# The gate columns of a mixer as seven products per quad, with turned queries cast later

## The chip, the cores and the metric

One core of one Trainium2 chip. The metric is the device time of one execution in microseconds; the kernel before takes 2320.2 us (median of 3 runs, 2319.61 to 2320.4).

## The reference, cut to what matters

Two layers over 512 tokens of 1024 features, all in f32; the kernel holds everything turned (features on the 128 partitions, tokens along the columns). The change lies in the mixer:

```python
u = rmsnorm(h, mix_norm[i])
b_g, c_g, v_c, q_c, kv_c, k_r, g_conv, g_mla = jnp.split(u @ w_in[i], split_pts, axis=-1)
#   widths:  512, 512, 512, 384, 256, 64, 1024, 1024
z = c_g * v_c                                   # short_conv_branch: three taps along the tokens
y = conv_w[0] * z[t-2] + conv_w[1] * z[t-1] + conv_w[2] * z[t]
y_conv = (b_g * y) @ w_conv_out                 # 512 -> 1024
y_mla = mla_branch(q_c, kv_c, k_r, ...)         # norms of q_c and kv_c, rotary parts, 8 heads
merged = jax.nn.sigmoid(g_conv) * y_conv + jax.nn.sigmoid(g_mla) * y_mla
h = h + merged @ w_o[i]
```

Each layer has a feed-forward block before the mixer and one behind it, and a gated per-layer input at its end.

## The kernel before

**Precision and form of a product.** Every f32 operand is split into two fp32r tiles, a high part (a cast on ScalarE, L67 for weights and L190 for activations) and a low part (source minus high part, on VectorE, L68 and L191). A product is then three matmuls (`mm3`, L196): high x high, high x low, low x high. Weights come as halves of 128 x 1024 f32 (512 KB, eight tiles of 128 x 128) through SyncE's queue into one of ten buffers `st` (`Stream.raw`, L45), and are split into one of four pairs `wh`/`wl` (`Stream.split`, L61).

**The mixer** (`mixer`, L517) is written in the order: norm of h and split into `xs` (eight pairs of 128 x 512); projections of kv, of the rotary key and of q; r, the reciprocal root mean square, by which each projection is multiplied on its way out of PSUM; norm and split of kv and the rotary key; then, for four blocks of 128 channels, projections C, V and B (`m0Cp`, `m0Vp`, `m0Bp`), with the tap loop behind them: z = V x C and y x b are multiplied on POOL (L578, L587), the first tap on VectorE (L581). Then come norm and split of q, eight rounds of one gate projection (`m0gcp`, 24 matmuls of 512 columns) and one output of the convolution (`m0cop`, 12), and eight more gate projections (`m0gmp`). Each gate is multiplied by r on VectorE and goes through the sigmoid on ScalarE. Behind the gates the attention runs over four pairs of heads: `qkv` (L608) makes the turned query `q_rope` (L628, its two casts L634 and subtractions L635 right behind it), keys, queries and values; `scores` (L653) and `turn` (L678) follow one pair later.

**The feed-forward block** (`ffn`, L375) computes its gate and up columns by a Strassen form in Winograd's variant: a quad of four weight quarters (`Quad`, L111) and seven half-size products (`step`, L440; `product`, L418). `Halved` (L346) holds the halves of the activations and their sums and differences (tiles `t` and `u`), split like all others. A product is 24 matmuls of 256 columns into a PSUM bank a, b or c; products 1, 6, 7 and 4 gather in bank b, 5 and 3 in c. ScalarE copies a bank out behind products 1, 5 and 6, VectorE adds behind 2, 3 and 7. `Quad.part` (L119) makes the sums of weight quarters on VectorE (L127 to L138) ahead of the split.

**What sets the order.** The code is written in one order; a scheduler of the tile framework then orders the instructions of each engine, allots the buffers of each pool and sets the waits. So the order on an engine is read from the built program. Names there: `wl`, `wh`, `st`, `s` are weights; `m0` and `m1` the mixers of the two layers; `h1` in `m0h1` the second pair of heads.

Of the kernel before, what the change touches and what calls it, by code (L numbers as in the profile page):

```python
# [158 lines left out]
def trunk_kernel(ctx, tc, dims, x, p, positions, gains, rope_c, weights, out):  # L159
# [186 lines left out]
    class Halved:  # L346
# [6 lines left out]
        def row(self, j, xs):  # L353
# [19 lines left out]
            halves_of(split(t24, f"{name}u{j}"), 6, 4)  # L373

    def ffn(l, nm, name, first=False, beside=None, early=False):  # L375
        H = S // 2
# [33 lines left out]


        def quad(n):
            quarters = {f"a{a_ + 1}{b_ + 1}": [(nm + "_w_gu", l, (4 * b_ + k) * P, c0 + (2 * n + a_) * P)
                                               for k in range(4) for c0 in (0, DFF)]
                        for a_ in range(2) for b_ in range(2)}
            todo[n] = {"w": Quad(W, quarters)}

        def product(ps, n, j):  # L418
            hi, lo = todo[n]["w"].part(j)
            for k, (vh, vl) in enumerate(ys[j]):  # L420
                for w in range(2):
                    at = slice((2 * k + w) * P, (2 * k + w + 1) * P)
                    for i, (a_, b_) in enumerate(((hi, vh), (hi, vl), (lo, vh))):
                        nc.tensor.matmul(ps[:, w, :], a_[:, at], b_, start=j in (1, 5, 2) and w + k + i == 0,
                                         stop=w + k + i == 6, skip_group_check=True)

# [12 lines left out]

        def step(n, j):  # L440
            if n not in todo:
                quad(n)
            d = todo[n]
            nn = f"{name}{n}"

            def T(what):
                return G(nn + what).rearrange("p (w t) -> p w t", t=H)

            bank = {1: "b", 6: "b", 7: "b", 4: "b", 5: "c", 3: "c", 2: "a"}[j]
            if j in (1, 5, 2):  # L450
                d[bank] = PS(nn + bank).rearrange("p (w t) -> p w t", t=H)
            ps = d[bank]
            product(ps, n, j)
            if j in (1, 5, 6):
                d[j] = T(f"c{j}")
                nc.scalar.copy(d[j], ps)
            elif j == 4:
                finish(n, 1, 0, ps, T("t"))
            else:
                i, f, c = {2: (1, 0, 0), 3: (6, 0, 1), 7: (5, 1, 1)}[j]  # L460
                nc.vector.tensor_tensor(d[i], ps, d[i], ALU.add)
                finish(n, f, c, d[i], d[i])

# [53 lines left out]
    def mixer(l):  # L517
# [82 lines left out]
        for m in range(KD):  # L600
            ps = proj(W.col("w_in", l, o_gm + m * P, D), xs, f"{name}gmp{m}")
            g = G(f"{name}gm{m}")
            nc.vector.tensor_tensor(g, ps, r, ALU.mult)  # L603
            nc.scalar.activation(g, g, AF.Sigmoid)
            m_b.append(g)
# [295 lines left out]
```

## Time and profile before

| | |
|---|---|
| median of 3 runs | 2320.2 us |
| the profiled execution: time, span | 2319.08 us, 2317.3 us |
| granted TensorE clock | 0.996 |
| busy: TensorE, its weight load, VectorE, ScalarE, POOL | 2294.0, 2051.2, 1791.4, 1064.2, 59.5 us |
| the gates of the first mixer | 451.32 to 560.15 us |
| the gates of the second mixer | 1592.54 to 1701.37 us |
| bytes read from HBM | 223.66 MB, 97 GB/s over the span |

Times of rows are microseconds from the span's start. Busy times of matmuls overlap, since they are pipelined: a record is 0.28 us long for 256 columns and 0.39 for 512, and what a matmul costs is the distance from one start to the next. Operations of VectorE overlap a little in the same way.

### The profile page before, as it was taken

Reading aid. Unit: us, or ns where it says so; the run is one execution under the profiler, and the core shown is the slowest. Engines: PE = TensorE matmul, PEld = TensorE weight load, DVE = VectorE, ACT = ScalarE, POOL = GpSimd, SP = SyncE. Lnnn points to the kernel's source line nnn. Section 1 sums busy time; section 2 is a strip of 40 time slices with the busy share of each in tenths; the row PEclk is TensorE's granted clock in tenths of the full one; section 3 lists DMA queues with packets and bytes.
Section 4 is the critical chain, followed back from the end, with each engine's and each line's share of the span. In section 5 each row is a group of like instructions: output and inputs, shape, how many; then the busy total and the mean of one; then the engine's idle time right before and its main releaser. Section 6 shows DMA issues by size and latency. Waiting matters only on the chain.

```text
span 2317.3 us, 33585 instructions
## 1 busy us (share of the span) xinstructions
PE 2294.0 (99%) x13696; PEld 2051.2 (89%) x13696; DVE 1791.4 (77%) x2483; ACT 1064.2 (46%) x1563; POOL 59.5 (3%) x58
## 2 busy tenths in 40 slices
PE   9999999999999999999999999999999999999997
PEld 7999988888888999998899999888888889999987
DVE  8988779745866988877898787687378679888776
ACT  7444444234544644444564444433245355444455
POOL 0000000200100000000000000001001000000000
PEclk9999999999999999999999999999999999999998
DMA  5333233332122233333223333322321213233341
GB/s 192 112 107 107 94 123 109 100 99 93 37 71 84 74 112 99 109 108 129 73 83 110 102 100 119 119 91 100 101 82 37 82 55 114 98 108 107 120 137 38
DMA packets 64523, 227.94 MB, mean 98 GB/s; under 512 B 7408, under 2 KB 7408, under 8 KB 64368
## 3 DMA queue, kind: packets, MB, share of 16 engines
q1 hardware_dynamic: 63936, 225.47, 29.7%
q8 instruction: 107, 1.75, 0.3%
q14 instruction: 48, 0.39, 0.1%
q10 hardware_dynamic: 432, 0.32, 0.0%
HBM read 223.66 MB, written 2.10 MB: 97 GB/s over the span
## 4 chain that ended last, share of the span: by engine, by line
PE 94%; DVE 4%; ACT 1%; issue 1%; DMA 0%; ACTq 0%; SPq 0%
PE a1pd L198 2%; PE b0pd L198 2%; PE b1pd L198 2%; PE a0pd L198 2%; PE b1pd L199 2%; PE b0pd L199 2%; PE a0pd L199 2%; PE a1pd L199 2%; PE a0pd L200 2%; PE a1pd L200 2%; PE b1pd L200 2%; PE b0pd L200 2%; DVE wl L68 1%; PE e1gp L198 1%; PE e1gp L199 1%; PE e1gp L200 1%
## 5 line engine op out<-in xcount | busy, mean ns | idle before, releaser
L67 ACT CAST wh<-st 128x1024 fp32r<-128x1024 f32 (+1 forms) x463 | 482.6, 1043 | 683.7 <-issue 146.3
L68 DVE TENSOR_TENSOR wl<-st,wh 128x1024 fp32r<-128x1024 f32 (+1 forms) x463 | 568.8, 1229 | 168.9 <-ACT wh L67 167.4
L67 ACT CAST wh<-s 128x1024 fp32r<-128x1024 f32 x78 | 81.9, 1050 | 101.0 <-PE b1pd L199 8.5
L68 DVE TENSOR_TENSOR wl<-s,wh 128x1024 fp32r<-128x1024 f32 x78 | 94.9, 1216 | 0.9 <-ACT wh L67 0.9
L135 DVE TENSOR_TENSOR st<-st,s 128x1024 f32<-128x1024 f32 x39 | 47.7, 1222 | 1.0
L138 DVE TENSOR_TENSOR st<-st,st 128x1024 f32<-128x1024 f32 x39 | 47.5, 1217 | 0.1
L132 DVE TENSOR_TENSOR s<-s,st 128x1024 f32<-128x1024 f32 x39 | 47.5, 1218 | 0.0
L127 DVE TENSOR_TENSOR s<-st,st 128x1024 f32<-128x1024 f32 x39 | 47.4, 1216 | 0.1
L469 DVE SCALAR_TENSOR_TENSOR h<-b0pd,h 128x512 f32<-128x512 f32 x40 | 27.5, 688 | 9.1 <-PE b0pd L200 9.1
L469 DVE SCALAR_TENSOR_TENSOR h<-b1pd,h 128x512 f32<-128x512 f32 x40 | 27.5, 688 | 9.1 <-PE b1pd L200 9.1
L469 DVE SCALAR_TENSOR_TENSOR h<-a1pd,h 128x512 f32<-128x512 f32 x40 | 27.5, 687 | 7.1 <-PE a1pd L200 7.0
L469 DVE SCALAR_TENSOR_TENSOR h<-a0pd,h 128x512 f32<-128x512 f32 x40 | 27.5, 687 | 6.4 <-PE a0pd L200 6.4
L103 POOL MEMSET wh<- 128x256 f32 x4 | 1.1, 312 | 1196.0 <-DVE wl L68 1196.0
L603 DVE TENSOR_TENSOR m1gm<-m1gmp,m1r 128x512 f32<-128x512 f32 x8 | 5.5, 691 | 26.5 <-PE m1gmp L200 26.5
L603 DVE TENSOR_TENSOR m0gm<-m0gmp,m0r 128x512 f32<-128x512 f32 x8 | 5.5, 691 | 26.2 <-PE m0gmp L200 26.2
L595 DVE TENSOR_TENSOR m1gc<-m1gcp,m1r 128x512 f32<-128x512 f32 x8 | 5.4, 689 | 11.3 <-PE m1gcp L200 11.3
L595 DVE TENSOR_TENSOR m0gc<-m0gcp,m0r 128x512 f32<-128x512 f32 x8 | 5.4, 689 | 11.3 <-PE m0gcp L200 11.3
L598 DVE TENSOR_TENSOR m0gc<-m0cop,m0gc 128x512 f32<-128x512 f32 x8 | 5.4, 690 | 8.4 <-PE m0cop L200 8.3
L598 DVE TENSOR_TENSOR m1gc<-m1cop,m1gc 128x512 f32<-128x512 f32 x8 | 5.4, 691 | 8.4 <-PE m1cop L200 8.3
L729 DVE TENSOR_TENSOR m1gm<-m1mop,m1gm 128x512 f32<-128x512 f32 x8 | 5.5, 690 | 6.6 <-PE m1mop L200 6.5
L729 DVE TENSOR_TENSOR m0gm<-m0mop,m0gm 128x512 f32<-128x512 f32 x8 | 5.5, 690 | 6.6 <-PE m0mop L200 6.5
L272 ACT ACT_TABLE_LOAD x8 | 10.3, 1283 | 0.1
(10023 smaller groups left out, 8593.3 us busy)
## 6 DMA issues: line engine op xcount, KB each, us to landing
st<-in_weights SPq DMA_DIRECT2D x416, 512.0 KB, 3.5
st<-in_weights SPq DMA_DIRECT2D x8, 256.0 KB, 5.3
h<-in_x SPq DMA_DIRECT2D x8, 256.0 KB, 5.4
out<-fo SPq DMA_DIRECT2D x8, 256.0 KB, 2.3
e0pi<-in_p SPq DMA_DIRECT2D x2, 256.0 KB, 3.7
e1pi<-in_p SPq DMA_DIRECT2D x2, 256.0 KB, 3.8
pos_i<-in_positions ACTq DMA_DIRECT2D x1, 256.0 KB, 4.4
cols<-in_gains ACTq DMA_DIRECT2D x1, 53.0 KB, 3.0
```

The costliest lines, as they stand in the source:

```text
L67: self.nc.scalar.copy(hi[:, w], src[:, w])
L68: self.nc.vector.tensor_tensor(lo[:, w], src[:, w], hi[:, w].bitcast(F32), ALU.subtract)
L127: tt(self.s, self.a21, self.a22, ALU.add)
L132: tt(self.s, self.s, self.a11, ALU.subtract)
L135: tt(self.a12, self.a12, self.s, ALU.subtract)
L138: tt(self.a11, self.a11, self.a21, ALU.subtract)
L198: nc.tensor.matmul(ps, wh, vh, start=first, stop=False)
L199: nc.tensor.matmul(ps, wh, vl, start=False, stop=False)
L200: nc.tensor.matmul(ps, wl, vh, start=False, stop=last)
L469: nc.vector.scalar_tensor_tensor(h[m], ps, 0.5, h[m], ALU.mult, ALU.add)
L603: nc.vector.tensor_tensor(g, ps, r, ALU.mult)
L729: nc.vector.tensor_tensor(t, mla_ps[m], t, ALU.mult)
```

## The change

It takes the seven-product form out of `ffn` into a class `Sevens` that the feed-forward block and the mixer use, and makes all 16 blocks of gate columns (2048 columns, `o_gc` and `o_gm` follow each other) by four quads of it. The halves of the activations for it (`ys`) are made one row per round of the convolution. The eight outputs of the convolution stand between products of quads 1 to 3. In the last quad the products stand in the order 6, 2, 7, 3, 4 in place of 2, 6, 3, 7, 4; the splits of q, kv and the rotary key, which stood at their norms, come behind its product 7. In the convolution C is multiplied by r squared, V by that product (both on VectorE, straight from PSUM), the first tap moves to ScalarE, y x b moves from POOL to VectorE, and q's norm moves from behind the loop into it. In `qkv` the casts of the turned query come behind the first key and query. The pool of activation tiles grows from 58 to 60 buffers.

```diff
-N_BIG = 58
+N_BIG = 60
...
+    class Sevens:
+        H = S // 2
+        BANK = {1: "b", 6: "b", 7: "b", 4: "b", 5: "c", 3: "c", 2: "a"}
...
+        def step(self, n, j):
...
+            ps = d[bank]
+            self.product(ps, d, j)
+            if j in (1, 5, 6):
+                d[j] = T(f"c{j}")
+                nc.scalar.copy(d[j], ps)
+            elif j == 4:
+                self.done(n, 1, 0, ps, T("t"))
+            else:
+                i, f, c = {2: (1, 0, 0), 3: (6, 0, 1), 7: (5, 1, 1)}[j]
+                nc.vector.tensor_tensor(d[i], ps, d[i], ALU.add)
+                self.done(n, f, c, d[i], d[i])
...
-        kvc = lat_norm(*kvt, "kv")
-        krh, krl = split(rope(krn, cosT, sinT, name + "kr"), name + "kr")
+        kvt = lat_norm(*kvt, "kv")
+        krt = rope(krn, cosT, sinT, name + "kr")
+        ys = Halved("mix", l, name)
...
+        r2 = G(name + "r2")
+        nc.vector.tensor_tensor(r2, r, r, ALU.mult)
         for k in range(CONV // P):
...
-            nc.vector.tensor_tensor(c, ps, r, ALU.mult)
+            nc.vector.tensor_tensor(c, ps, r2, ALU.mult)
...
-            nc.vector.tensor_tensor(z, ps, r, ALU.mult)
-            nc.gpsimd.tensor_tensor(z, z, c, ALU.mult)
+            nc.vector.tensor_tensor(z, ps, c, ALU.mult)
...
-            nc.vector.tensor_scalar(y, z, cw[2], None, ALU.mult)
+            nc.scalar.mul(y, z, cw[2])
...
-            nc.gpsimd.tensor_tensor(y, y, b, ALU.mult)
+            nc.vector.tensor_tensor(y, y, b, ALU.mult)
             yc.append(split(y, f"{name}yc{k}"))
+            ys.row(k, xs)
+            if k == 1:
+                qt = lat_norm(*qt, "q", SCALE)
...
+        def gate(n, f, c, src, t):
+            at = slice(c * (S // 2), (c + 1) * (S // 2))
+            nc.vector.tensor_tensor(t, src, r[:, at].unsqueeze(1).to_broadcast([P, 2, S // 2]), ALU.mult)
+            for w in range(2):
...
+                nc.scalar.activation(gates[i][:, at], t[:, w, :], AF.Sigmoid)
...
+        step = Sevens("w_in", l, name + "g", ys.ys,
+                      lambda n: [[o_gc + (4 * n + 2 * a_ + w) * P for w in range(2)] for a_ in range(2)], gate).step
+        for j in (1, 2, 5, 6, 3):
+            step(0, j)
+        n_last = KD // 2 - 1
+        for n in range(n_last):
+            between = [(lambda m=m: conv_out(m)) for m in range(4 * n - 4, 4 * n)] if n else []
+            order = [(n + 1, 1), (n, 7), (n + 1, 5), (n, 4)]
+            order += [(n + 1, j) for j in ((6, 2, 7, 3, 4) if n + 1 == n_last else (2, 6, 3))]
+            for i, (n_, j_) in enumerate(order):
+                step(n_, j_)
+                if i in (1, 2, 3, 4 if n + 1 == n_last else 5) and between:
+                    between.pop(0)()
+                if (n_, j_) == (n_last, 7):
+                    qc = [split(t, f"{name}qn{k}") for k, t in enumerate(qt)]
+                    kvc = [split(t, f"{name}kvn{k}") for k, t in enumerate(kvt)]
+                    krh, krl = split(krt, name + "kr")
...
             for _, part in parts:
                 part()
+                if part is query0:
+                    q_rope_parts()
```

Three places of VectorE's order in the first mixer (the second has the same). The first is the edge from the convolution to the gates, in the changed kernel; `m0b` is B times r, `m0y` the tap loop's sum, `m0t` and `m0u` half sums, `s` and `st` weight quarters:

```order
L601 TENSOR_TENSOR m0b_4330<-m0Bp_4299,m0r 128x512
L68 TENSOR_TENSOR wl_4464<-s,wh_4463 128x1024
L602 TENSOR_TENSOR m0y_4295<-m0y_4295,m0b_4330 128x512
L138 TENSOR_TENSOR st_4355<-st_4355,st_4357 128x1024
L191 TENSOR_TENSOR m0yc3l<-m0y_4295,m0yc3h 128x512
L68 TENSOR_TENSOR wl_4495<-st_4361,wh_4494 128x1024
L368 TENSOR_TENSOR m0t_4339<-m0x_4337 128x256
L369 TENSOR_TENSOR m0t_4339<-m0y_4338,m0x_4337 128x256
L68 TENSOR_TENSOR wl_4536<-st_4526,wh_4535 128x1024
L370 TENSOR_TENSOR m0u_4340<-m0t_4339,m0x_4337 128x256
L371 TENSOR_TENSOR m0u_4340<-m0y_4338,m0u_4340 128x256
L191 TENSOR_TENSOR m0t3l<-m0t_4339,m0t3h 128x512
```

Before, the convolution's edge had only its own rows, two weight splits and q's norm; now sums of quarters and splits of the first two quads stand among them, and the last half sums behind them.

The second place is the end of the gates, in the changed kernel (`m0g3` is the last quad, `m0qn`, `m0kvn` and `m0kr` the late splits):

```order
L191 TENSOR_TENSOR m0qn0l<-m0qt_3794,m0qn0h 128x512
L424 TENSOR_TENSOR m0g3c_5292<-m0g3c,m0g3c_5292 128x512
L191 TENSOR_TENSOR m0qn1l<-m0qt_3798,m0qn1h 128x512
L613 TENSOR_TENSOR m0g3c_5292<-m0g3c_5292,m0r 128x512
L191 TENSOR_TENSOR m0qn2l<-m0qt_3803,m0qn2h 128x512
L68 TENSOR_TENSOR wl_5591<-st_5588,wh_5590 128x1024
L191 TENSOR_TENSOR m0kvn0l<-m0kvt_3682,m0kvn0h 128x512
L68 TENSOR_TENSOR wl_5736<-st_5733,wh_5735 128x1024
L191 TENSOR_TENSOR m0kvn1l<-m0kvt_3686,m0kvn1h 128x512
L191 TENSOR_TENSOR m0krl<-m0krt_3826,m0krh 128x512
L613 TENSOR_TENSOR m0g3t<-m0g3b,m0r 128x512
```

The three kinds of late splits moved here from the convolution and the first gates; two memsets and the turned query's first row follow.

The third place is the second pair of heads, before:

```order
L68 TENSOR_TENSOR wl_5617<-st_5614,wh_5616 128x1024
L514 TENSOR_TENSOR m0h1qrt_5229<-m0h1qrt_5229,m0h1qrt_5230 128x512
L635 TENSOR_TENSOR m0h1qr_5237<-m0h1qrt_5229,m0h1qr_5237 64x512
L635 TENSOR_TENSOR m0h1qr_5240<-m0h1qrt_5229,m0h1qr_5240 64x512
L191 TENSOR_TENSOR m0h1kn0l<-m0h1kn_5243,m0h1kn0h 128x512
L191 TENSOR_TENSOR m0h1qn0l<-m0h1qn_5254,m0h1qn0h 128x512
L191 TENSOR_TENSOR m0h1kn1l<-m0h1kn_5274,m0h1kn1h 128x512
```

and in the changed kernel:

```order
L191 TENSOR_TENSOR m0h1kn0l<-m0h1kn_5715,m0h1kn0h 128x512
L529 TENSOR_TENSOR m0h1qrt_5707<-m0h1qrt_5707,m0h1qrt_5708 128x512
L191 TENSOR_TENSOR m0h1qn0l<-m0h1qn_5726,m0h1qn0h 128x512
L68 TENSOR_TENSOR wl_6027<-st_6024,wh_6026 128x1024
L674 TENSOR_TENSOR m0h1qr_5746<-m0h1qrt_5707,m0h1qr_5746 64x512
L674 TENSOR_TENSOR m0h1qr_5749<-m0h1qrt_5707,m0h1qr_5749 64x512
L191 TENSOR_TENSOR m0h1kn1l<-m0h1kn_5752,m0h1kn1h 128x512
```

Between the sum of the turned query (`qrt`) and the subtractions that need ScalarE's cast of it, the first query's split and a weight split have moved.

## Rows read from the trace of the kernel before

**Rows 1.** The page: busy time, share of the span and instructions of each engine, and the chain that ended last by engine.

```profile
PE 2294.0 (99%) x13696; PEld 2051.2 (89%) x13696; DVE 1791.4 (77%) x2483; ACT 1064.2 (46%) x1563; POOL 59.5 (3%) x58
...
PE 94%; DVE 4%; ACT 1%; issue 1%; DMA 0%; ACTq 0%; SPq 0%
```

**Rows 2.** The waits of TensorE: who waited <- for whom: us in total, times, longest.

```profile
PE a0pg L198 <- ACT a0x0h L193: 5.3, 1, 5.3
PE fss L808 <- DVE f0acc L259: 2.6, 1, 2.6
...
PE m0s10p L664 <- DVE m0h1v0l L191: 0.6, 1, 0.6
...
PE m0s20p L664 <- DVE m0h2kn1l L191: 0.3, 1, 0.3
...
PE m0s30p L664 <- DVE m0h3kn1l L191: 0.3, 1, 0.3
```

**Rows 3.** The first mixer's convolution, gates and attention in stretches: the stretch, its us, then busy us (instructions) of PE, PEld, DVE, ACT and POOL, granted clock, DMA share, GB/s.

```profile
385.55:451.32 65.77, 65.77 (x291) 54.43 (x290) 51.18 (x62) 19.30 (x24) 11.53 (x7) 1.00 0.28 94
451.32:560.15 108.83, 108.83 (x481) 90.09 (x480) 51.33 (x56) 32.93 (x41) 1.29 (x1) 1.00 0.30 99
560.15:655.40 95.25, 93.92 (x556) 83.66 (x554) 85.19 (x207) 56.68 (x135) 14.94 (x16) 1.00 0.16 50
```

**Rows 4.** The timeline of TensorE at the first gate matmul and at the first of the turned query, in both layers: start, us, engine, line, operation, tiles, shape.

```profile
451.32 0.39 PE L198 MATMUL m0gcp<-m0x0h,wh 128*128 128x512 f32 x1
...
560.15 0.39 PE L198 MATMUL m0h0qr<-m0qn0h,wh 128*128 128x512 f32 x1
...
1592.54 0.39 PE L198 MATMUL m1gcp<-m1x0h,wh 128*128 128x512 f32 x1
...
1701.37 0.39 PE L198 MATMUL m1h0qr<-m1qn0h,wh 128*128 128x512 f32 x1
```

**Rows 5.** The timeline of TensorE in the second feed-forward block of the first layer: the first matmul of the first product of its first quad, and of the ninth and the twelfth product; then one weight load of such a product (duration min/median/max in ns).

```profile
769.77 0.28 PE L424 MATMUL b01b<-b0x0h,wh 128*128 128x256 f32 x1
...
794.18 0.28 PE L424 MATMUL b01b<-b0u0h,wh 128*128 128x256 f32 x1
...
802.82 0.28 PE L424 MATMUL b02c<-b0x4h,wh 128*128 128x256 f32 x1
```

```profile
L424 PEld LDWEIGHTS b01b<-b0u0h,wh x4: 192/192/192, 778.3 to 794.4; 128*128 128x128 f32 x4
```

**Rows 6.** The timeline of VectorE in the same block: rows of 512, 1024 and 256 columns, each with the next.

```profile
801.26 0.68 DVE L461 TENSOR_TENSOR b02c<-b02a,b02c 128x512 f32<-128x512 f32 x1
801.86 1.21 DVE L68 TENSOR_TENSOR wl<-st,wh 128x1024 fp32r<-128x1024 f32 x1
802.99 0.68 DVE L431 TENSOR_TENSOR b02c<-b02c,b0r 128x512 f32<-128x512 f32 x1
...
804.73 0.42 DVE L436 TENSOR_TENSOR b0an<-b02c 128x256 f32<-128x256 f32 x1
805.07 1.22 DVE L127 TENSOR_TENSOR s<-st,st 128x1024 f32<-128x1024 f32 x1
```

**Rows 7.** ScalarE by line and shape between 764 and 800 us: count | busy us, mean ns of one | idle before.

```profile
L67 ACT CAST wh<-st 128x1024 fp32r<-128x1024 f32 x7 | 7.3, 1047 | 2.5 <-PE b01a L424 0.8 <-DVE st L138 0.8 <-DVE st L135 0.8
L432 ACT ACTIVATE b01c<-b01c 128x256 f32<-128x256 f32 x3 | 1.3, 418 | 2.8 <-DVE b01c L431 2.8
L456 ACT COPY b01c<-b01b 128x512 f32<-128x512 f32 x2 | 1.2, 579 | 0.0
L364 ACT ACTIVATE b0x<-h,cols 128x512 f32<-128x512 f32 x1 | 0.7, 717 | 0.0
```

**Rows 8.** The page's DMA issues: count, KB each, median us from issue to landing.

```profile
st<-in_weights SPq DMA_DIRECT2D x416, 512.0 KB, 3.5
```

**Rows 9.** VectorE by line and shape in the first mixer's convolution (385.55 to 451.32); then one weight split there, and POOL's timeline beside it.

```profile
L68 DVE TENSOR_TENSOR wl<-st,wh 128x1024 fp32r<-128x1024 f32 x12 | 17.9, 1489 | 0.9 <-ACT wh L67 0.8
L273 DVE RECIPROCAL m0kvr<-m0kvt 128x512 f32<-128x512 f32 x1 | 3.3, 3341 | 0.0
```

```profile
446.52 2.30 DVE L68 TENSOR_TENSOR wl<-st,wh 128x1024 fp32r<-128x1024 f32 x1 [0.21 <-ACT wh L67]
```

```profile
446.45 1.29 POOL L578 TENSOR_TENSOR m0z<-m0z,m0c 128x512 f32<-128x512 f32 x1 [9.59 <-DVE m0z L577]
```

**Rows 10.** The timeline of VectorE: the wait for ScalarE's cast of y, and two rows of which the second needs the first.

```profile
417.12 0.69 DVE L191 TENSOR_TENSOR m0yc0l<-m0y,m0yc0h 128x512 fp32r<-128x512 f32 x1 [1.83 <-ACT m0yc0h L190]
...
459.84 0.69 DVE L275 SCALAR_TENSOR_TENSOR m0qt<-m0qt,m0qms 128x512 f32<-128x512 f32 x1
460.56 0.69 DVE L276 SCALAR_TENSOR_TENSOR m0qr<-m0qt,m0qr 128x512 f32<-128x512 f32 x1
```

**Rows 11.** The timeline of VectorE and of TensorE in the second pair of heads of the first mixer.

```profile
587.36 1.41 DVE L635 TENSOR_TENSOR m0h1qr<-m0h1qrt,m0h1qr 64x512 fp32r<-64x512 f32 x2 [0.69 <-ACT m0h1qr L634]
...
592.33 0.68 DVE L191 TENSOR_TENSOR m0h1v0l<-m0h1v,m0h1v0h 128x512 fp32r<-128x512 f32 x1
```

```profile
593.15 0.41 PE L664 MATMUL m0s10p<-m0h1kn0h,m0h1qn0h 128*128 128x384 f32 x1 [0.61 <-DVE m0h1v0l L191]
```

**Rows 12.** The timeline of TensorE at the scores of the first pair of heads.

```profile
572.00 0.28 PE L665 MATMUL m0s00p<-m0h0kn0l,m0h0qn0h 128*128 128x256 f32 x1
572.12 0.28 PE L666 MATMUL m0s00p<-m0h0kn0h,m0h0qn0l 128*128 128x256 f32 x1
```

More of the change, by code (lines that the diff above doesn't have):

```diff
@@ L373, in row, with __init__, quad, product @@
             halves_of(split(t24, f"{name}u{j}"), 6, 4)
+    class Sevens:
+        H = S // 2
+        BANK = {1: "b", 6: "b", 7: "b", 4: "b", 5: "c", 3: "c", 2: "a"}
+        def __init__(self, w, l, name, ys, columns, done):
+            self.w, self.l, self.name, self.ys, self.columns, self.done = w, l, name, ys, columns, done
+            self.todo = {}
+        def quad(self, n):
+            cs = self.columns(n)
+            quarters = {f"a{a_ + 1}{b_ + 1}": [(self.w, self.l, (4 * b_ + k) * P, c) for k in range(4) for c in cs[a_]]
+                        for a_ in range(2) for b_ in range(2)}
+            return {"w": Quad(W, quarters)}
+        def product(self, ps, d, j):
+            hi, lo = d["w"].part(j)
+            for k, (vh, vl) in enumerate(self.ys[j]):
+                for w in range(2):
+                    at = slice((2 * k + w) * P, (2 * k + w + 1) * P)
+                    for i, (a_, b_) in enumerate(((hi, vh), (hi, vl), (lo, vh))):
+                        nc.tensor.matmul(ps[:, w, :], a_[:, at], b_, start=j in (1, 5, 2) and w + k + i == 0,
+                                         stop=w + k + i == 6, skip_group_check=True)
+        def step(self, n, j):
+            if n not in self.todo:
+                self.todo[n] = self.quad(n)
+            d = self.todo[n]
+            nn = f"{self.name}{n}"
+            def T(what):
+                return G(nn + what).rearrange("p (w t) -> p w t", t=self.H)
+            bank = self.BANK[j]
+            if j in (1, 5, 2):
+                d[bank] = PS(nn + bank).rearrange("p (w t) -> p w t", t=self.H)
+            ps = d[bank]
[9 more added lines that the diff above has]
+                self.done(n, f, c, d[i], d[i])
     def ffn(l, nm, name, first=False, beside=None, early=False):
@@ L379, in ffn @@
         acts = {}
-        todo = {}
-        hv = Halved(nm, l, name)
+        ys = Halved(nm, l, name)
         n_early = KD // 2 - 2 if early else 0
@@ L385, in early_rows @@
             if KD // 2 < k + 1 <= KD // 2 + n_early:
-                hv.row(k - KD // 2, xs)
+                ys.row(k - KD // 2, xs)
         xs, acc = normed(nm, l, name, early_rows)
@@ L399, in ffn @@
         for j in range(n_early, KD // 2):
-            hv.row(j, xs)
-        ys = hv.ys
+            ys.row(j, xs)
         def activate(f):
@@ L409, in activate @@
             acts[f] = split(u, f"{name}a{f}")
[L412 to L425, printed above, removed]
         def finish(n, f, c, src, t):
@@ L438, in finish @@
                 acts[i] = split(acts[i], f"{name}a{i}")
[L440 to L462, printed above, removed]
+        sevens = Sevens(nm + "_w_gu", l, name, ys.ys, lambda n: [[c + (2 * n + a_) * P for c in (0, DFF)] for a_ in range(2)],
+                        finish)
+        step = sevens.step
         def down(m, f0, f1, ps=None, last=True, first_=True):
@@ L600, in mixer @@
[L600 to L605, printed above, removed]
+            ys.row(k, xs)
+            if k == 1:
+                qt = lat_norm(*qt, "q", SCALE)
+        gates = [None] * (2 * KD)
+        def gate(n, f, c, src, t):
+            at = slice(c * (S // 2), (c + 1) * (S // 2))
+            nc.vector.tensor_tensor(t, src, r[:, at].unsqueeze(1).to_broadcast([P, 2, S // 2]), ALU.mult)
+            for w in range(2):
+                i = 4 * n + 2 * f + w
+                if gates[i] is None:
+                    gates[i] = G(f"{name}g{i}")
+                nc.scalar.activation(gates[i][:, at], t[:, w, :], AF.Sigmoid)
@@ L608, in qkv @@
+        m_a, m_b = gates[:KD], gates[KD:]
         def qkv(pr):
@@ L644, in query @@
                 res["qn", t] = split(ps, f"{n}qn{t}")
-            parts = [(3, q_rope), (2, lambda: key(0)), (3, lambda: query(0)), (2, lambda: key(1)), (3, lambda: query(1))]
+            query0 = lambda: query(0)
+            parts = [(3, q_rope), (2, lambda: key(0)), (3, query0), (2, lambda: key(1)), (3, lambda: query(1))]
             at = [i for i in range(1, len(parts) + 1) if W.pairs_fit(2, sum(w for w, _ in parts[:i]))]
```

19 lines of the change are left out of this document (6 added, 13 removed).

## The prediction

> **What bounds the kernel now.** I read the page first. TensorE is busy 99% of the span, and the chain that ended last lies 94% on it [rows 1]. The list of TensorE's waits comes next, because only these and the pitch of its matmuls can change the time: they sum to some 16 us, most of it at the kernel's start and end, and the mixer's share is 1.2 us a layer [rows 2]. Last come the windows of the three stretches of the mixer that the change touches (convolution, gates, attention), all at the full granted clock of 1.00 [rows 3]. In the gates TensorE is busy for all of 108.83 us and VectorE for 51.33, so that stage is paid in matmuls. From its first gate matmul to the first matmul of the turned query it takes 560.15 - 451.32 = 108.83 us, and 1701.37 - 1592.54 = 108.83 us in the second layer [rows 4]. It has 16 x 24 + 8 x 12 = 480 matmuls of 512 columns: 226.7 ns each, without a gap.
>
> **Fewer columns.** Four quads of seven products, each 24 matmuls of 256 columns, make 672; the 96 of the convolution's output stay. The feed-forward block has the same products: from the start of its ninth, 794.18, to that of its twelfth, 802.82, TensorE runs three of them without a gap, so one takes 2.88 us and a matmul of 256 columns 120 ns [rows 5]. After: 28 x 2.88 = 80.64, plus 96 x 0.2267 = 21.77, makes 102.41. **Term 1: -6.42 us a layer.** It is less than the eighth that the arithmetic saves (16 x 5.44 / 8 = 10.9), since two short matmuls take 240 ns where one long one took 227.
>
> The Trainium skill ("TensorE: Matmul & The Clock Gate", Back-to-back issue gap) gives N/2.4 + 2.5 ns, 109.2 and 215.8 ns here. By it, term 1 would be an estimated -9.5 us; both rows lie about 11 ns above it, so the measurement decides.
>
> **VectorE and ScalarE in the gates.** Consecutive VectorE starts lie 1.13 us apart behind an operation of 1024 columns and 0.60 behind one of 512 [rows 6]. A layer's gates need 32 weight splits and 16 additions of quarters (48 x 1.13 = 54.2), and 12 additions of products, 16 multiplications by r, 8 by the gate and 6 late splits (42 x 0.61 = 25.6): 80 of 102 us. ScalarE: 32 casts of 1.05, 12 copies of 0.58, 32 sigmoids of 0.42 [rows 7], and 6 casts like the copies: 58 us. Both fit. The twenty loads of 512 KB a layer remain; they land in 3.5 us at a DMA share of 0.30 [rows 3, 8], and the feed-forward block already loads quads four at a time.
>
> **The convolution, where VectorE gets tight.** It loses the multiplication by the third tap (to ScalarE) and gains r squared, the product that POOL did, the four rows of half sums, and the q norm that stood in the gates. Weight splits there averaged 1489 ns: 2.30 us for one at 446.52 beside POOL's multiplication from 446.45 [rows 9], 1.21 in the feed-forward block [rows 6]. With POOL's eight operations gone I price them at 1.13. The order of the changed kernel has, from b1 to just ahead of b3, 9 rows of 1024, 27 of 512, 8 of 256 (0.34 each, [rows 6]) and one reciprocal of 3.3 [rows 9]: 10.2 + 16.5 + 2.7 + 3.3 = 32.7 us. About 17 of them wait for a row just ahead; such a pair starts 0.72 apart, not 0.60 [rows 10], so 1.7 to 2 more: 34.6. TensorE's two rounds take 2 x 72 x 0.2267 plus 0.45 for q's sum of squares: 33.1. VectorE is then 1.5 us late at b3. Nine rows lead from there to the split for the second quad's first product: 4 x 1.13 + 3 x 0.61 + 2 x 0.34 = 7.0; TensorE wants it after 68 matmuls, 8.2 us. So 7.0 + 1.5 + about 0.6 for handovers = 9.1 against 8.2. **Term 2: +1.0 us a layer** (0 if gaps absorb the dependences; 2.8 if one turnaround through ScalarE, 1.83 at 417.12 [rows 10], comes on top). Behind this split on VectorE stand the last half sums, wanted 1.4 us later; they slip with it, not again. As a check, the feed-forward block's start of quads: product 1 at 769.77, and the twelfth, 11 x 2.88 = 31.7 us later if dense, at 802.82 [rows 5], so 1.4 us lost.
>
> **The end of the gates.** The splits of q, kv and the rotary key now stand behind product 7 of the last quad. Between its end and the key's last split VectorE has about 8 x 0.61 + 3 x 1.13 = 8.3 us; TensorE has two products, 9 matmuls and a few more, about 8.5. **Term 3: +0.3** (0 to 1.0).
>
> **The attention.** Before, VectorE waits 0.69 us at 587.36 for ScalarE's cast of the turned query, v0's split then starts at 592.33, and TensorE waits 0.61 for it at 593.15 [rows 11]; the next two pairs cost 0.3 each [rows 2]. With the casts behind key and query that gap closes. Against it, two more splits stand ahead of the turned query than before, so VectorE enters the attention 1.2 us later. **Term 4: -0.3** (-1.2, all three waits gone, to +1.5, the lag passed on). The table loads of ScalarE keep their number, and outside the mixers nothing is reordered.
>
> **Sum.** -6.42 + 1.0 + 0.3 - 0.3 = -5.42 a layer, -10.84 in all. The profiled execution took 2319.08 (span 2317.3): 2308.2. The median is 1.1 above it: **2309.4 us**.
>
> **Rivals.** About 0.2%, 4.6 us, can be told from no change.
>
> *The convolution becomes VectorE's.* There is no slack to speak of: from the kv norm to b3 it has 16 rows of 1024, 52 of 512, 12 of 256, 4 of the rotary key at 0.7 and 2 reciprocals, 63.4 us, and some 66 with the dependences, against 66 of TensorE. If ScalarE's turnarounds (y by the third tap, y's cast) show each time, as 1.83 us did at 417.12 [rows 10], with 0.7 more for the tap's own time [rows 7], that is 4 x 2.5 = 10 us a layer in place of term 2's 1.0: +3.6 a layer, 2327. It decides when waits there pass 7.7 us a layer more than I forecast. Against it, the order puts b between the product and the tap, and quarter sums or splits ahead of the cast's partner. Chance 6%.
>
> *Half of that:* 3 to 7.7 us a layer more is waited at the two edges of the gates and in the attention; at 5 it is 2319, no change. Chance 13%. Between this and the forecast, with 1.8 to 3 us more, lie 2313 to 2315.6: 12%.
>
> *Matmuls cost by column alone*, and the 120 ns comes from the feed-forward block: half of 226.7 is 113.3, term 1 becomes 97.9 - 108.83 = -10.9, the time 2300.4. Against it, the attention's 256-column matmuls also stand 0.12 apart [rows 12]. 2%.
>
> *Each weight load is paid.* 288 more matmuls bring 288 more loads; at the load's own record of 192 ns [rows 5], 55 us a layer are added, and -10.9 + 55 makes 2409. But a matmul follows the last in 120 ns, less than its load's record, so loads overlap. 1%. The Trainium skill (same page, Part 3, The mechanism) says that a load overlaps running matmuls only in another row group, which full 128-row weights never are; its 107 ns a load would make an estimated +20 us a layer, and the rows contradict it.
>
> **How the numbers follow.** The forecast's own case, 2305 to 2313, has 66%: terms 2 to 4 at their kind ends give -7.6 a layer, 2305.0, and at the dear ends together 2318, of which I keep the part up to 2316. The range 2304.5 to 2316 holds that case, the 12% beside it and a little of no change: eight in ten. Faster: 66 + 12 + 2 = 80%; same 13%; slower 7%.
>
> **What would show it.** In the profile after: 672 matmuls of 256 columns a mixer at a pitch of 120 ns, and from the first gate product to the turned query 103 to 105 us. TensorE's waits should name the first products of the second quad (or t3's half sums) with about 1 us, and no v0 split in the second pair. Weight splits in the convolution should average 1.22 us. The forecast is wrong if TensorE waits inside the convolution's projections, if a product's pitch is not 2.88, or if the gates' quads wait one after another for VectorE.

## The result and the profile after

The changed kernel takes 2305.06 us (median of 6 runs, 2304.29 to 2305.56), the kernel before 2320.3 in the same rounds: 15.2 us less, a ratio of 0.9935 with a 95% interval of 0.9922 to 0.9948. The forecast was 2309.4, 10.8 below the 2320.2 on record, in a range of 2304.5 to 2316. So the sign and the range hold, and the gain is larger than forecast by 4.3 us. The profiled execution took 2305.14, its span 2303.4.

The page's busy times and chain, answering [rows 1]:

```profile
PE 2281.0 (99%) x14272; PEld 2068.1 (90%) x14272; DVE 1881.2 (82%) x2613; ACT 1129.3 (49%) x1683; POOL 36.8 (2%) x42
...
PE 93%; DVE 5%; ACT 1%; issue 1%; DMA 0%; ACTq 0%; SPq 0%
```

TensorE's waits, answering [rows 2] (who <- for whom: us in total, times, longest):

```profile
PE m0s10p L706 <- DVE m0h1qn1l L191: 0.9, 1, 0.9
PE m1s10p L706 <- DVE m1h1qn1l L191: 0.9, 1, 0.9
```

These are the only waits of a mixer in the list: none at the edge from the convolution to the gates, none at the gates' end. The stretches, answering [rows 3] (us, then busy us of PE, PEld, DVE, ACT, POOL, granted clock, DMA share, GB/s), and the stage's ends, answering [rows 4]:

```profile
386.24:452.04 65.80, 65.80 (x291) 54.43 (x290) 64.31 (x87) 27.50 (x37) 0.00 (x0) 1.00 0.18 56
452.04:554.85 102.81, 102.81 (x769) 98.69 (x768) 80.17 (x92) 55.40 (x83) 0.00 (x0) 1.00 0.39 123
554.85:648.79 93.94, 92.92 (x557) 83.21 (x555) 88.10 (x211) 57.83 (x138) 16.08 (x15) 1.00 0.18 57
```

```profile
452.04 0.28 PE L400 MATMUL m0g0b<-m0x0h,wh 128*128 128x256 f32 x1
...
554.85 0.40 PE L198 MATMUL m0h0qr<-m0qn0h,wh 128*128 128x512 f32 x1
...
1586.12 0.28 PE L400 MATMUL m1g0b<-m1x0h,wh 128*128 128x256 f32 x1
...
1688.92 0.40 PE L198 MATMUL m1h0qr<-m1qn0h,wh 128*128 128x512 f32 x1
```

Gates: 102.81 and 102.80 us in place of 108.83. Attention: 93.94 and 93.95 in place of 95.20 and 95.33 (the next stage of the first layer begins at 655.35, 0.05 ahead of the end of the stretch in [rows 3]). The convolution keeps its time (65.80), but VectorE is now busy for 64.31 of it, before for 51.18 [rows 3].

At the edge TensorE hardly stands, though VectorE is late, because the order of its matmuls weaves two products. TensorE, then VectorE, at the first quad's third product (bank `m0g0c`) and the second quad's first (`m0g1b`):

```profile
459.96 0.28 PE L400 MATMUL m0g1b<-m0x0h,wh 128*128 128x256 f32 x1
460.08 0.28 PE L400 MATMUL m0g1b<-m0x0l,wh 128*128 128x256 f32 x1
460.33 0.38 PE L400 MATMUL m0g1b<-m0x0h,wl 128*128 128x256 f32 x1
460.55 0.28 PE L400 MATMUL m0g1b<-m0x0h,wh 128*128 128x256 f32 x1
...
461.86 0.28 PE L400 MATMUL m0g0c<-m0t3l,wh 128*128 128x256 f32 x1
```

```profile
453.05 0.69 DVE L601 TENSOR_TENSOR m0b<-m0Bp,m0r 128x512 f32<-128x512 f32 x1
...
459.06 1.22 DVE L68 TENSOR_TENSOR wl<-st,wh 128x1024 fp32r<-128x1024 f32 x1
...
460.99 0.68 DVE L191 TENSOR_TENSOR m0t3l<-m0t,m0t3h 128x512 fp32r<-128x512 f32 x1
```

Row 3 of the third product waits for `m0t3l`, done at 461.67; until 461.86 TensorE runs almost only the second quad's matmuls, whose weights are split from 459.06 to 460.28. The first matmul that needs this split (460.33) starts 0.25 us behind the one ahead, and the next one 0.22, where the pitch is 0.12: 0.23 us are lost here, in pauses too short for the list of waits.

### The profile page after: what moved, and what is told of

The parts are those of the page before. It is cut to its first block, busy times and chain, and to the rows that moved or that the text cites. A ratio compares the mean times of both kernels' runs of the same rounds, so it can differ in the third digit from the quotient of the medians.

```text
span 2303.4 us, 34969 instructions
## 1 busy us (share of the span) xinstructions
PE 2281.0 (99%) x14272; PEld 2068.1 (90%) x14272; DVE 1881.2 (82%) x2613; ACT 1129.3 (49%) x1683; POOL 36.8 (2%) x42
## 4 chain that ended last, share of the span: by engine, by line
PE 93%; DVE 5%; ACT 1%; issue 1%; DMA 0%; ACTq 0%; SPq 0%
PE a0pd L198 2%; PE b0pd L198 2%; PE b1pd L198 2%; PE a1pd L198 2%; PE a1pd L199 2%; PE b0pd L199 2%; PE a0pd L199 2%; PE b1pd L199 2%; PE a1pd L200 2%; PE b1pd L200 2%; PE a0pd L200 2%; PE b0pd L200 2%; DVE wl L68 1%; PE e1gp L198 1%; PE e1gp L199 1%; PE e1gp L200 1%
## 5 line engine op out<-in xcount | busy, mean ns | idle before, releaser
L67 ACT CAST wh<-st 128x1024 fp32r<-128x1024 f32 (+1 forms) x471 | 490.8, 1043 | 588.0 <-issue 66.4
L67 ACT CAST wh<-s 128x1024 fp32r<-128x1024 f32 x94 | 98.8, 1051 | 120.2 <-PE b0pd L199 8.5
L68 DVE TENSOR_TENSOR wl<-s,wh 128x1024 fp32r<-128x1024 f32 x94 | 114.4, 1217 | 13.4 <-ACT wh L67 13.3
L135 DVE TENSOR_TENSOR st<-st,s 128x1024 f32<-128x1024 f32 x47 | 57.4, 1222 | 1.1
L132 DVE TENSOR_TENSOR s<-s,st 128x1024 f32<-128x1024 f32 x47 | 57.3, 1218 | 0.2
L138 DVE TENSOR_TENSOR st<-st,st 128x1024 f32<-128x1024 f32 x47 | 57.2, 1217 | 0.1
L127 DVE TENSOR_TENSOR s<-st,st 128x1024 f32<-128x1024 f32 x47 | 57.1, 1216 | 0.1
L771 DVE TENSOR_TENSOR m0g<-m0mop,m0g 128x512 f32<-128x512 f32 x8 | 5.5, 691 | 6.5 <-PE m0mop L200 6.5
L824 ACT ACTIVATE e_0g<-e_0g 128x512 f32<-128x512 f32 (+1 forms) x13 | 6.8, 529 | 2.8 <-DVE e_0g L823 2.7
L861 PE MATMUL ft<-ident,fh 128*128 128x128 f32 x32 | 5.9, 322 | 1.8 <-DVE fh L853 1.8
```

The lines of the kernel that those rows point to most:

```text
L67: self.nc.scalar.copy(hi[:, w], src[:, w])
L68: self.nc.vector.tensor_tensor(lo[:, w], src[:, w], hi[:, w].bitcast(F32), ALU.subtract)
L127: tt(self.s, self.a21, self.a22, ALU.add)
L132: tt(self.s, self.s, self.a11, ALU.subtract)
L135: tt(self.a12, self.a12, self.s, ALU.subtract)
L138: tt(self.a11, self.a11, self.a21, ALU.subtract)
```

## The experiments

Each is the changed kernel with one edit, timed in five rounds beside the kernel before on the same chip. "Edge" is the convolution's end and the first gate products; the pairs of heads are counted from the first. All tables of stages come from TensorE's first matmul of each.

**The gates as before, all else changed.**

```diff
-        step = Sevens("w_in", l, name + "g", ys.ys, ...)
+        for m in range(KD):                      # gate(): 24 matmuls of 512 columns
+            gates[m] = gate(o_gc, m, "gc")
...
+        for m in range(KD):
+            gates[KD + m] = gate(o_gm, m, "gm")
+            if m == KD - 3:                      # the late splits
...
```

> The changed kernel with the gates as before: sixteen projections of 24 matmuls of 512 columns, no half sums, no sums of weight quarters; the convolution, the late splits (behind the sixth gate from the end) and the turned query's casts stay as changed. Theory A (the parts add up): TensorE's time from the first gate matmul to the turned query is 108.8 us again instead of 102.8, the attention keeps its 93.9, the convolution its 65.8: 2305.1 + 2 x 6.0 = 2317.1 us, and about 3 us below the kernel before. Rival B (the gain of the attention comes from the gates' new end and not from the casts): the attention is at 95.2 again, 2319.8, no difference from before.

2313.01 us, 6.9 below before (ratio 0.9972, 0.9962 to 0.9983). Gates 108.8, convolution 65.8: by itself, the convolution's rewriting does not change the convolution's time. But the attention takes 92.0, below what either theory had, and TensorE is busy through all of it:

```profile
560.26:652.25 91.99, 91.99 (x555) 83.21 (x554) 85.49 (x207) 57.27 (x135) 15.82 (x16) 1.00 0.16 52
```

So the changed attention can be 3.2 us a layer shorter than before, and the changed kernel gives 1.9 of it back. Both expectations missed that. This run does not say whether the new gates or the place of the late splits takes the 1.9: here the splits stand two gates ahead of the end and are done 4.9 us before the attention begins. The runs below that move the splits settle it.

**The casts at their old place.**

```diff
                 res["qr"] = rope(ps, cosT, sinT, n + "qr")
+                q_rope_parts()
...
-                if part is query0:
-                    q_rope_parts()
```

> The changed kernel with the turned query's casts and subtractions right behind its sum again, as before; all else as changed. Theory A (VectorE's three waits of 0.7 us a layer for ScalarE's cast were what the attention lost): they come back, TensorE waits again ahead of the second, third and fourth pair, and the attention takes 95.2 us a layer (as before) to 96.4 (with 1.2 us of VectorE's lag from the late splits on top) in place of 93.9: 2307.7 to 2310. Rival B (the attention gained by other places of its weight splits): no change, 2305.1 within 0.5.

2318.14 us (0.9993, 0.9984 to 1.0002): 13 us lost, far beyond Theory A's 5. In the profiled execution, which took 2316.36, the four pairs take 21.1, 26.5, 25.3 and 26.6 (changed: 18.3, 26.1, 24.3, 25.3), 5.5 us a layer; the 1.8 us by which the median lies above it stand in no trace. In the first pair VectorE comes late, then stands for ScalarE's cast, with the first key's and query's splits behind it, and TensorE waits 2.0 us for the first scores:

```profile
566.20 1.40 DVE L675 TENSOR_TENSOR m0h0qr<-m0h0qrt,m0h0qr 64x512 fp32r<-64x512 f32 x2 [0.74 <-ACT m0h0qr L674]
567.64 0.69 DVE L191 TENSOR_TENSOR m0h0kn0l<-m0h0kn,m0h0kn0h 128x512 fp32r<-128x512 f32 x1
```

**The late splits back at their norms.**

```diff
         kvt = lat_norm(*kvt, "kv")
+        kvc = [split(t, f"{name}kvn{k}") for k, t in enumerate(kvt)]
         krt = rope(krn, cosT, sinT, name + "kr")
+        krh, krl = split(krt, name + "kr")
...
                 qt = lat_norm(*qt, "q", SCALE)
+                qc = [split(t, f"{name}qn{k}") for k, t in enumerate(qt)]
...
-                if (n_, j_) == (n_last, 7):      # and the three late splits below it
```

> The changed kernel with the splits of q, kv and the rotary key back at their norms in the convolution: six subtractions, 6 x 0.61 = 3.7 us of VectorE, stand ahead of the first two quads' weights again. Theory A (VectorE has 1.5 us free of 65.8 in the convolution, so it has no room): the edge from the convolution to the gates slips by 2 to 3.6 us, TensorE waits for it at the second quad's first product or at the last half sums, and the end of the gates gives nothing back: 2309 to 2312. Rival B (the order of TensorE, which mixes the first quad's third product with the second quad's first, takes up the delay): 2305 to 2306.

2315.3 us (0.9981, 0.9972 to 0.9990). The gates take 109.4 and 110.0, so the edge lost 6.6 and 7.1 from 3.7 us more of VectorE's work: Theory A's place, at twice its price. Two things multiply it. The last channel block's chain, which began at 446.99 in the changed kernel, falls behind sums and splits of the next quads and comes at 456.51 (first fence); and behind TensorE's wait of 3.93 us (second) the granted clock stands at 0.59 over four microseconds (third), its lower level of 1.2 GHz for most of them, where matmuls follow each other in 0.21 us and not 0.12.

```profile
452.70 1.22 DVE L138 TENSOR_TENSOR st<-st,st 128x1024 f32<-128x1024 f32 x1
...
454.77 1.22 DVE L68 TENSOR_TENSOR wl<-s,wh 128x1024 fp32r<-128x1024 f32 x1
...
456.51 0.69 DVE L592 TENSOR_TENSOR m0c<-m0Cp,m0r 128x512 f32<-128x512 f32 x1
```

```profile
467.06 0.38 PE L400 MATMUL m0g0c<-m0t3h,wh 128*128 128x256 f32 x1 [3.93 <-ACT m0t3h L190]
467.93 0.58 PE L400 MATMUL m0g0c<-m0t3l,wh 128*128 128x256 f32 x1 [0.49 <-DVE m0t3l L191]
...
470.24 0.41 PE L400 MATMUL m0g0b<-m0u0h,wl 128*128 128x256 f32 x1
470.45 0.41 PE L400 MATMUL m0g0b<-m0u1h,wh 128*128 128x256 f32 x1
```

```profile
468.00:472.00 4.00, 4.00 (x21) 4.00 (x22) 3.64 (x5) 3.31 (x5) 0.00 (x0) 0.59 0.15 55
472.00:476.00 4.00, 4.00 (x36) 4.00 (x35) 3.79 (x4) 2.77 (x5) 0.00 (x0) 1.00 0.22 32
```

The waits are 4.4 us of the 6.6 in the first layer; the slow clock is most of the rest. The second pair of heads takes 24.2 us here, not 26.1, and the attention 92.0: without the late splits VectorE enters the attention on time. So the end of the gates does give something back, which Theory A had at nothing.

**Both multiplications of the convolution on POOL.**

```diff
-            nc.vector.tensor_tensor(c, ps, r2, ALU.mult)
+            nc.vector.tensor_tensor(c, ps, r, ALU.mult)
...
-            nc.vector.tensor_tensor(z, ps, c, ALU.mult)
+            nc.vector.tensor_tensor(z, ps, r, ALU.mult)
+            nc.gpsimd.tensor_tensor(z, z, c, ALU.mult)
...
-            nc.vector.tensor_tensor(y, y, b, ALU.mult)
+            nc.gpsimd.tensor_tensor(y, y, b, ALU.mult)
```

> The changed kernel with both multiplications of the convolution on POOL again (C and V each times r on VectorE, their product and y times b on POOL); the first tap stays on ScalarE. VectorE then has four operations of 512 columns less, 2.4 us a layer. Theory A (a weight split beside a POOL operation takes 2.3 us in place of 1.2, and the chain waits for POOL): the twelve weight splits average 1.5 us again, 3.3 us a layer more than now, and with VectorE waiting for POOL's results of 1.3 us each the edge of the gates is 1 to 3 us late: 2307 to 2311. Rival B (POOL's work costs VectorE nothing that matters, and 2.4 us are free): no change or 0.5 us less, 2304.5 to 2305.3.

2327.71 us (1.0033, 1.0021 to 1.0046), slower than before: the gates' stretch takes 114.3 and 113.4, 11.5 and 10.6 more, nearly four times Theory A's upper price. Its mechanism was half wrong. The weight splits are not stretched (1219 ns on average). VectorE stands, 6.8 us in four stops for the tap on ScalarE, which waits for POOL's product. TensorE then waits 8.9 us at the edge of the first layer, and its granted clock stands at 0.50 for over 5 us behind that, which is most of the other 2.6.

**Only y times b on POOL.** The last line of the diff above, alone.

> The changed kernel with only y times b on POOL again, one of the two multiplications of a channel block, at the end of its chain; C times V stays on VectorE. VectorE has 2.4 us a layer less to do. Theory A (with both on POOL the edge of the gates was 11 us longer because C times V heads the chain: VectorE stood 6.8 us idle for the tap that waits for POOL): VectorE does not stand for y times b, the edge is 0 to 2 us longer, 2305 to 2309. Rival B (the two engines slow each other, so each POOL operation costs the same): half of it, 5 to 6 us a layer, 2315 to 2317.

2320.05 us (1.0002, 0.9993 to 1.0010): the whole gain is gone, with gates of 110.4 and 109.8. Theory A fell: this multiplication alone costs 7.6 and 7.0 us of the 11.5 and 10.6 of both, so by difference more than the other, which was not run alone. Rival B was nearer in size. In the first layer TensorE's waits at the edge are 4.8 us of the 7.6; behind them its clock stands at 0.50 for some 6 us, most of the other 2.8. POOL's four rows, and VectorE's beside the second and the third:

```profile
409.12 3.26 POOL L602 TENSOR_TENSOR m0y<-m0y,m0b 128x512 f32<-128x512 f32 x1 [47.31 <-DVE m0y L598]
422.48 1.30 POOL L602 TENSOR_TENSOR m0y<-m0y,m0b 128x512 f32<-128x512 f32 x1 [10.10 <-DVE m0y L598]
440.54 3.28 POOL L602 TENSOR_TENSOR m0y<-m0y,m0b 128x512 f32<-128x512 f32 x1 [16.76 <-DVE m0y L598]
456.30 3.26 POOL L602 TENSOR_TENSOR m0y<-m0y,m0b 128x512 f32<-128x512 f32 x1 [12.48 <-DVE m0b L601]
```

```profile
422.85 2.01 DVE L68 TENSOR_TENSOR wl<-st,wh 128x1024 fp32r<-128x1024 f32 x1
...
440.31 1.22 DVE L68 TENSOR_TENSOR wl<-st,wh 128x1024 fp32r<-128x1024 f32 x1
441.45 1.22 DVE L127 TENSOR_TENSOR s<-st,st 128x1024 f32<-128x1024 f32 x1
444.50 0.69 DVE L191 TENSOR_TENSOR m0yc2l<-m0y,m0yc2h 128x512 fp32r<-128x512 f32 x1 [1.83 <-ACT m0yc2h L190]
```

The two engines take turns. At 422.48 POOL is first, takes 1.30, and VectorE's split is stretched to 2.01. At 440.54 VectorE is first: POOL ends 3.28 later, at 443.82, which is the end of VectorE's sum, 442.67, and 1.15 more; and VectorE then stands 1.83 us for the cast of POOL's result. Three such stops are 5.5 us, the wait that [rows 10] showed before. The Trainium skill ("SBUF — State Buffer", SBUF: two separate sides) says that these two engines share a port pair under an exclusive lock, taken by a VectorE operation with two inputs in SBUF or by POOL's, and that the later one blocks until the earlier is done. These rows agree in that the later one waits, 3.28 against 1.30 us; but POOL, whose row begins at 440.54, waited also for the sum that VectorE began at 441.45.

**The first tap back on VectorE.**

```diff
-            nc.scalar.mul(y, z, cw[2])
+            nc.vector.tensor_scalar(y, z, cw[2], None, ALU.mult)
```

> The changed kernel with the convolution's first tap on VectorE again, four operations of 0.48 us, 1.9 us a layer; all else as changed. Theory A (VectorE's lag at the edge of the gates is multiplied, since the last channel block's chain falls behind weight work of the next quads: 3.7 us more of work made the edge 6.6 to 7.2 us longer): 2 to 4 us a layer, 2309 to 2313. Theory B (only the work beyond the free 0.5 us counts): 1 to 1.5 us a layer, 2307 to 2308. Rival C (the hop to ScalarE and back that falls away pays for it): 2305.

2307.9 us (0.9949, 0.9937 to 0.9962), gates 104.3 in both layers: 1.4 us a layer, with a wait of 1.05 us for the second quad's split and a clock that stays at 1.00. Theory B held: by this difference VectorE has about half a microsecond to spare there, and this wait is not multiplied.

**The last quad in the old order.**

```diff
-            order += [(n + 1, j) for j in ((6, 2, 7, 3, 4) if n + 1 == n_last else (2, 6, 3))]
+            order += [(n + 1, j) for j in ((2, 6, 3, 7, 4) if n + 1 == n_last else (2, 6, 3))]
```

> The changed kernel with the last gate quad's products in the order 2, 6, 3, 7, 4 in place of 6, 2, 7, 3, 4; all else as changed. Theory A (every product is 2.88 us and VectorE has 20% idle time there, so the order pays nothing by itself): 2305.1 within 0.7. Rival B (the order moves what stands behind the last products on VectorE, and with it the entry of the attention): product 7 and the late splits behind it come one product later, so the second pair loses up to 2 us a layer more: 2306.5 to 2309.

2307.78 us (0.9948, 0.9936 to 0.9961), gates 103.8 in both layers, the pairs unchanged. Rival B has the size about right and the place wrong:

```profile
553.30 0.39 PE L400 MATMUL m0g3b<-m0u0h,wh 128*128 128x256 f32 x1 [0.78 <-DVE m0g3c L424]
```

```profile
552.55 0.69 DVE L424 TENSOR_TENSOR m0g3c<-m0g3b,m0g3c 128x512 f32<-128x512 f32 x1 [0.25 <-PE m0g3b L400]
```

Products 7 and 4 gather in the same bank, so 4 must wait until VectorE has read it behind 7. In the changed order product 3 stands between them, in bank c. That is 1.02 us a layer, 2.0 of the 2.7 us between the two kernels, and the prediction did not see it at all.

**The late splits earlier in the gates.**

```diff
-                if (n_, j_) == (n_last, 7):
+                if (n_, j_) == (n_last - 1, 4):
```

> The changed kernel with the six late splits of q, kv and the rotary key seven of TensorE's steps earlier, behind product 4 of the third quad, where VectorE has idle time; all else as changed. Theory A (the attention of the changed kernel loses 1.9 us a layer in its second pair only because VectorE enters it late, with these splits behind it): the second pair takes 24.3 us as it does with the plain gates or with early splits, in place of 26.1, and the gates keep 102.8: 2305.1 - 2 x 1.85 = 2301.4. Rival B (the second pair loses it by the gates' last product, whatever stands behind): 26.1 stays, 2305.1. Rival C (the earlier splits make the third or fourth quad's weights late): gates over 103.5, 2304 to 2307.

2301.22 us (0.9921, 0.9907 to 0.9935), **the best kernel here**, at Theory A's number. The gates keep 102.8, the second pair takes 24.2 in both layers, the attention 92.0, and the list has no wait of TensorE left in a mixer. So the place of the late splits took the 1.9 us, and the new gates none. VectorE's first row of the turned query before, in the changed kernel (with the last split ahead of it) and here, while TensorE begins the attention at 560.15, 554.85 and 555.14:

```profile
562.40 0.69 DVE L510 TENSOR_TENSOR m0h0qrt<-m0h0qr,cosT 128x512 f32<-128x512 f32 x1
```

```profile
558.50 0.68 DVE L191 TENSOR_TENSOR m0krl<-m0krt,m0krh 128x512 fp32r<-128x512 f32 x1
...
559.99 0.62 DVE L525 TENSOR_TENSOR m0h0qrt<-m0h0qr,cosT 128x512 f32<-128x512 f32 x1
```

```profile
557.49 0.68 DVE L525 TENSOR_TENSOR m0h0qrt<-m0h0qr,cosT 128x512 f32<-128x512 f32 x1
```

VectorE comes 2.25 us behind TensorE before, 5.14 in the changed kernel and 2.35 here.

**The old casts with the earlier splits.** Both diffs together.

> The changed kernel with the late splits behind product 4 of the third quad (as in the run before with 2301.2) and with the turned query's casts right behind its sum again. Theory A (the casts' old place costs 3.2 us a layer by itself, the difference of the attention between the kernel before, 95.2, and plain gates with the new casts, 92.0; the other 2.4 us that it cost in the changed kernel came from meeting VectorE's lag in the first pair): the pairs take 18.2, 25.4, 25.3 and 26.3 us as before, 2301.2 + 6.4 = 2307.6. Rival B (the old place costs 5.6 us a layer whatever VectorE's lag): the first pair at 21.1, 2312.4.

2308.25 us (0.9951, 0.9937 to 0.9964). The pairs take 18.2, 25.4, 25.3 and 26.6. Theory A held within 0.7 us: the casts' place alone is worth 7.0 us, 3.5 a layer.

**The mixer's last projection by two quads of seven.**

```diff
-            ps = proj(W.col("w_o", l, m * P, D), merged, f"{name}wop{m}")
-            nc.vector.tensor_tensor(h[m], ps, h[m], ALU.add)
+        step = Sevens("w_o", l, name + "w", wy.ys, lambda n: [[(4 * n + 2 * a_ + w) * P ...]], add).step
+        for n, j in ((0, 1), (0, 2), (0, 5), (0, 6), (0, 3), (1, 1), (0, 7), ...):
+            step(n, j)
```

> The changed kernel with the mixer's last projection (1024 to 1024 columns) by two quads of seven products as well: 14 x 2.88 = 40.3 us in place of 192 x 0.2267 = 43.5. Theory A (TensorE's pitch decides, VectorE is idle for 36 of 92 us from the attention's output projection to the mixer's end): 2 to 3.2 us a layer less, 2298.7 to 2301.1. Rival B (the last rows of h come together at the end and the next norm waits for them, or the last half sums are late at the third product): 0 to 1 us a layer less, 2303 to 2305.

2328.53 us (1.0038, 1.0026 to 1.0051). Both theories missed: the projection itself becomes longer, and the feed-forward block behind it loses more. From the first matmul of the projection, of the block, and of its first quad, until the first output product: first the changed kernel, then this one.

```profile
697.43:740.95 43.52, 43.52 (x193) 36.04 (x192) 26.73 (x32) 17.76 (x23) 0.00 (x0) 1.00 0.26 85
740.95:763.20 22.25, 22.25 (x99) 18.40 (x98) 21.14 (x31) 15.72 (x23) 0.00 (x0) 1.00 0.08 25
763.20:804.92 41.72, 41.07 (x337) 40.47 (x336) 41.25 (x56) 25.61 (x36) 0.00 (x0) 1.00 0.34 104
```

```profile
697.83:741.10 43.27, 40.80 (x313) 40.07 (x312) 38.31 (x56) 22.44 (x30) 0.00 (x0) 0.92 0.36 117
741.10:766.84 25.74, 25.48 (x124) 21.24 (x124) 25.74 (x38) 17.84 (x26) 0.00 (x0) 1.00 0.15 49
766.84:817.43 50.59, 43.64 (x337) 42.12 (x336) 48.24 (x66) 29.71 (x43) 0.00 (x0) 0.97 0.32 95
```

```profile
706.45 0.38 PE L404 MATMUL m0w0a<-m0mg7l,wh 128*128 128x256 f32 x1 [1.15 <-DVE m0mg7l L191]
...
708.37 0.58 PE L404 MATMUL m0w1b<-m0mg0h,wh 128*128 128x256 f32 x1 [1.06 <-ACT wh L67]
...
742.96 0.39 PE L404 MATMUL m0w1b<-m0wu0h,wh 128*128 128x256 f32 x1 [0.26 <-DVE m0w1c L428]
```

```profile
708.00:712.00 4.00, 3.37 (x13) 3.06 (x14) 4.00 (x7) 1.95 (x4) 0.00 (x0) 0.50 0.68 209
```

The first of these stretches does not hold the whole projection: its last product, 24 matmuls of 2.96 us from 742.96 on, stands behind the block's first matmuls, in the second stretch. So the projection takes about 46.2 us where 43.5 were spent before and 40.3 expected: TensorE waits 1.15 us for the last split of its operand and 1.06 for weights, and behind these two waits its clock stands at 0.50 for some 7 us. The block's start then loses about 0.6 us and its first quad 8.9; in the quad TensorE stands for 6.95 of 50.59 us, where it stood for 0.65 of 41.72. VectorE was already busy for 21.14 of 22.25 us, then 41.25 of 41.72, at the block's start. That the rows of h, which now arrive late together, find no gap there is the likely reason, but no run separates it.

## Why the prediction was right, and where its sizes were off

| per layer | forecast | measured |
|---|---|---|
| term 1, fewer columns | -6.42 | -6.25 |
| term 2, the edge | +1.0 | +0.23 |
| term 3, the gates' end | +0.3 | 0 in the gates |
| term 4, the attention | -0.3 | -1.26 and -1.38: the casts -3.2, VectorE's late entry +1.9 |
| sum | -5.4 | -7.25 and -7.37, with 0.03 for the convolution |

The two layers make -14.6; the start of the program took 0.7 more (the first mixer's convolution begins at 386.24, before at 385.55), which leaves the spans' difference of 13.9. The profiled execution of before lay 1.2 below its median, the changed one on it, so the medians differ by 15.2.

*Term 1* is right: a product takes 2.88 us. Of the 0.40 us beyond 102.41, 0.23 are the pauses at the edge; the rest lies at the convolution's outputs, each of which takes 2.75 between products of 256 columns and took 2.72 before.

*Term 2* was sized 0.8 us too dear. The weight splits did fall to 1214 ns on average, as forecast, and B's last row comes at 453.05, 1.0 behind TensorE's end of the projections, not 1.5. The split is done 7.2 us later, 8.2 in all against the 8.2 wanted, without the 0.6 for handovers; only the 0.23 us above are lost. That little is left over is what the tap shows, where 1.9 us more cost 1.4.

*Term 3* named the right rows and the wrong payer. TensorE finishes the gates without a wait, but VectorE's lag goes on into the attention, where the second pair pays 1.9 us. Moving the splits takes just this away.

*Term 4* had both of its mechanisms and neither of their sizes. It let VectorE enter the attention 1.2 us later, by two splits; it enters 2.9 later (5.14 us behind TensorE, before 2.25), since the splits of kv and of the rotary key and one more weight split stand ahead. And it failed as a bound: the prediction took "all three waits gone, -1.2" for its kind end, from the list of waits [rows 2]. What the casts' old place cost was 3.2 us, or 3.5 in the run that moves nothing else. The list shows only a part: in the third pair before it has 0.27 us (0.3 in the list), yet the ten transposes ahead take 1.69 us from start to start, and 1.01 after:

```profile
615.58 1.42 PE L683 MATMUL m0t10t<-ident,m0s10e 128*128 128x128 f32 x10
617.27 0.39 PE L664 MATMUL m0s20p<-m0h2kn0h,m0h2qn0h 128*128 128x256 f32 x1 [0.27 <-DVE m0h2kn1l L191]
```

```profile
611.01 1.25 PE L725 MATMUL m0t10t<-ident,m0s10e 128*128 128x128 f32 x10
612.02 0.36 PE L706 MATMUL m0s20p<-m0h2kn0h,m0h2qn0h 128*128 128x256 f32 x1
```

In these views a pause that lies under a long or grouped record counts as busy.

*Luck* has a part in it. The measured sum lies near the sum of the prediction's kind ends, -7.6 a layer, because term 2 came out small and because the two halves of term 4, each larger than thought, partly cancel. Of the signs named, the weight splits' 1.2 us came, and 102.8 us of gates is just under the 103 to 105; the list of waits names nothing at the second quad, and in the second pair v0's split is gone, but the second query's (`m0h1qn1l`) stands in its place with 0.9 us.

*The rivals.* None came. The convolution did not become VectorE's, but the runs show how near it was: y times b on POOL alone brings the time back to 2320, by the stop for ScalarE's cast that the rival counted on, and with both multiplications there the gates' stretch grows by 11.5 us, near the rival's 10, though partly by the slow clock, which the rival did not have. Columns alone, and paid weight loads, are excluded by the product's 2.88 us.

## What to carry to other kernels

Price a wait by the distance between starts in a dense and a disturbed copy of the same stretch, not by the list of waits. Where an engine is 98% busy in front of a stage, the price of more work there need not grow in proportion: here 1.9 us cost 1.4 and 3.7 us cost 6.6 to 7.1. So move work that nobody waits for into the next stage's idle time, and not to its end, where it only makes the engine late for the one after. A form that saves TensorE's time by more work elsewhere paid here where the engine that gets the work had idle time (the gates), and did not where the stage behind had none (the last projection).

## What was not expected of the hardware

After TensorE had stood 3.9 us, its clock was granted at 1.2 GHz for some microseconds of work, at 0.21 us a matmul of 256 columns and not 0.12 (late splits at their norms). After a wait of 1.05 us it stayed at 1.00 (the tap); but behind two, of 1.15 and 1.06 us with a few matmuls between them, it stood at 0.50 for some 7 us (the last projection). So the length of one wait did not tell what the clock would do. And POOL's multiplication of 1.30 us took 3.28 beside a subtraction and a sum of VectorE, since it waited for both in a row.
